# Routing in a two-block transformer kernel: groups of u between the searches, six gather buffers, sums brought together by DMA, two stored batches kept in their tiles

## The chip, the core and the metric

The kernel runs on one core of a Trainium2 chip. The core has five engines with queues of their own: TensorE (PE), VectorE (DVE), ScalarE (ACT), GpSimd (POOL) and SyncE (SP), which here only issues DMAs. The metric is the time of one execution on the device in microseconds; a kernel is told by the median of several executions. Lower is better.

## What is computed

The kernel computes two blocks of a transformer on 512 tokens of width 1024, all in float32. The change touches the last part of the second block alone, a product-key mixture of 128 x 128 experts (`peer_ffn` of the reference):

```python
q = (xb @ w_pq).reshape(tokens, 8, 2, 128)
s = einsum("thpd,hpnd->thpn", q, sub_keys)          # 8 heads x 2 halves x 128 keys
s_top, i_top = top_k(s, 16)                         # per half
cand = s_top[:, :, 0, :, None] + s_top[:, :, 1, None, :]
best, ci = top_k(cand, 16)                          # 16 of the pairs
e = i1 * 128 + i2                                   # expert numbers, from i_top and ci
gate = softmax(best)
act = gelu(einsum("thkd,td->thk", u_exp[e], x))
y = einsum("thk,thkd->td", gate * act, v_exp[e])
out = rmsnorm(x_res + gt2 * y, final_g)
```

`u_exp` and `v_exp` have 16384 rows of 1024 numbers (64 MB each).

## The kernel before

**Two ways through the experts.** The first 128 tokens (`NS`) take a sparse way: for each of 4 groups of 32 tokens (`NG`) and 32 steps, an indirect DMA on the POOL queue gathers 128 rows of 4 KB from `u` (`sparse_u`, L1387) and later from `v` (`sparse_v`, L1678), and DVE multiplies and sums each gathered tile in one instruction (L1405 for u, L1697 for v). The other 384 tokens (`ND`) take a dense way: TensorE multiplies all of `u` with the tokens, ACT applies the gelu, the result is weighted with a matrix `W` that holds each token's gates at its experts (zero elsewhere), and TensorE multiplies that with all of `v`.

**Exact products.** A float32 product is made of three fp32r products of 128x384 or 128x512 (`mm3`, L194 to L196) of a high and a low part. ACT makes the high part (L148), DVE or POOL the low one by a subtraction (L149), both in `split`.

**A group of u** is one call of `expert_early` (L1417): `expert_parts` loads 512 KB of `u` through the SP queue (L1357) into one of three tiles `uraw` and splits it into `uhl` (three tiles of the tag "wlo"); `expert_u` runs 24 products and a gelu (L1366) into one quarter of a tile `ga`. There are 128 groups in 32 batches of four. A full `ga` is stored to `GAd` by the ACT queue (L1428) and loaded again later (L1650). Batch 31 (`N_EARLY`) isn't stored: it is computed at the start of the v stage. `ahead` holds the parts that are prepared early, here one group ahead of the products.

**The stages**, in the order of the program:

1. *Scores and searches* (to about 1294 us): products of `w_pq`; `top16` on DVE finds the 16 best of each half.
2. *Routing*, a loop over four tiles of 128 tokens (L1498): DVE builds the pairs `cand`, searches them (eight calls of `top16`, one for each head), takes differences for the softmax (L1522), ACT applies Exp (L1523), and eight rounds `h` of one-hot products `eq` (L1534, L1538) and sums (L1544) turn the found places into expert numbers `ei`. In six of the eight rounds (all but `H_SKIP`) one group of u is called, with POOL as the engine of the low part; four more (`E_LAST`) follow the loop. `pick` transposes `ei` and `gate` on TensorE, and DVE and ACT (L1489) copy them out. `share` sends both through DRAM for the sparse tokens after the first tile (L1380 to L1384).
3. *Marks*: 48 units of eight tokens. DVE (L1584) and ACT (L1585) make one-hot matrices from the picks, TensorE multiplies them (L1604), ACT copies the result to `stage`, which is stored to `Wd`. In each unit some two groups of u run and some three steps of `sparse_u` are taken, which the two `while` conditions at the end of the loop meter out. DVE makes the low parts here.
4. *v*: for each of 32 batches (`order`), `prepare` loads `W` (`Wt`, L1646), `ga` and 2 MB of `v` (L1656) and splits them; `products` runs 96 matmuls of 128x384 into eight banks of PSUM that stay open to the end. Between them `sparse_v` is stepped by a condition with `57`.
5. *End*: the last batch is multiplied bank by bank; after bank 3 the sparse tokens are ended. Their sums lie in `fin` on 128 partitions, four partitions for a token; eight matmuls with a 0/1 matrix `FOLD` (L1710) add the four. Then the norm and the output.

**Who sets the order.** The program is written in the tile language: a planner at build time puts the instructions of each engine in order by its own estimate of times, within the data dependences. `tc.keep_in_program_order` pins an instruction behind the one traced before it on the same engine. On the chip every engine and every DMA queue then runs strictly in that order, so an instruction that waits holds all behind it.

## Time and profile before

| what | value |
|---|---|
| median of three executions | 2561.01 us (2559.43 to 2565.94) |
| profiled execution, whole | 2564.41 us |
| its span, first to last instruction | 2562.4 us |
| busy: PE, DVE, ACT, POOL | 2452.3, 1753.2, 1159.9, 509.8 us |
| mean granted clock of TensorE | 0.979 of full speed |
| moved by DMA | 545.79 MB |

All rows below come from the profiled execution. A view by stretches shows for each engine its busy time and, in brackets, its instructions, then the granted clock and the DMAs' share of time and rate. A view of waits shows which instruction waited for which: in total, how often, and the longest. A timeline shows start, duration, engine, line, operation, written tile and read tiles, and in square brackets how long the engine had been idle and what ended that. All times are microseconds; "mean ns" is nanoseconds.

### The profile page before, as it was taken

What the parts mean: (1) busy time and instruction counts of PE and PEld (TensorE: products, weight loads), DVE (VectorE), ACT (ScalarE), POOL (GpSimd) and SP (SyncE); (2) the same over time, 40 slices, a digit from 0 to 9 for tenths busy, and PEclk for the clock granted to TensorE, in tenths of its full rate; (3) what the DMA queues carried; (4) which work ended last, traced back from release to release, by engine and by line L of the source; (5) the groups of instructions that cost most, each with busy time, mean ns of one, the idle gap of its engine ahead of it and who ended that gap; (6) DMA issues with size and microseconds to landing.
All of it is one profiled execution on the core that took longest, in us unless ns stands there. A gap on an engine that the chain in (4) does not pass through costs nothing.

```text
span 2562.4 us, 36881 instructions
## 1 busy us (share of the span) xinstructions
PE 2452.3 (96%) x13565; PEld 2241.0 (87%) x13565; DVE 1753.2 (68%) x4163; ACT 1159.9 (45%) x2339; POOL 509.8 (20%) x389
## 2 busy tenths in 40 slices
PE   8899989999999999999997889999999999999998
PEld 7789878888878888888896789999999899999997
DVE  6467687643374567446889777777773588888884
ACT  7346464323244445224232467767675333333333
POOL 0021000000000000000043344434420144445430
PEclk9899999999999999999998889999999999999999
DMA  8511347742332221334133589999996999999981
GB/s 299 183 63 34 112 154 274 256 171 91 107 131 104 94 87 65 111 132 160 62 101 101 169 323 345 351 345 335 338 332 232 332 340 365 366 370 359 367 302 58
DMA packets 181905, 545.79 MB, mean 213 GB/s; under 512 B 17259, under 2 KB 68003, under 8 KB 170972
## 3 DMA queue, kind: packets, MB, share of 16 engines
q1 hardware_dynamic: 130592, 353.52, 40.0%
q0 software_dynamic: 38944, 139.49, 14.6%
q10 hardware_dynamic: 12188, 50.44, 5.0%
q8 instruction: 106, 1.74, 0.3%
q14 instruction: 75, 0.61, 0.1%
HBM read 480.25 MB, written 67.33 MB: 214 GB/s over the span
## 4 chain that ended last, share of the span: by engine, by line
PE 71%; DVE 10%; issue 9%; POOL 5%; DMA 3%; ACT 2%; POOLq 0%; SPq 0%; DVEq 0%; ACTq 0%
PE bank L196 21%; PE bank L194 21%; PE bank L195 20%; POOL gu L1375 5%; DVE eq L1534 1%; PE bank L1604 1%; DMA gu<-in_u_rows,eS 1%; PE bank L732 1%; PE bank L324 1%; PE bank L735 1%; DVE best L1544 1%; PE bank L323 1%; DMA adaw<-in_w_adaT 1%; PE bank L1164 1%; DVE eq L1538 1%
## 5 line engine op out<-in xcount | busy, mean ns | idle before, releaser
L194 PE MATMUL bank<-hTh,uhl 128*128 128x384 f32 x1024 | 357.7, 349 | 33.8 <-ACT uhl L148 33.8
L196 PE MATMUL bank<-hTh,uhl 128*128 128x384 f32 x1024 | 355.0, 347 | 23.9 <-DVE uhl L149 12.3
L195 PE MATMUL bank<-hTl,uhl 128*128 128x384 f32 x1024 | 352.1, 344 | 0.0
L196 PE MATMUL bank<-wah,vlo 128*128 128x384 f32 x1024 | 347.2, 339 | 0.0
L194 PE MATMUL bank<-wah,vhi 128*128 128x384 f32 x1024 | 346.0, 338 | 0.0
L195 PE MATMUL bank<-wal,vhi 128*128 128x384 f32 x1024 | 344.7, 337 | 0.0
L194 PE MATMUL bank<-hTh,whi 128*128 128x512 f32 (+1 forms) x832 | 318.4, 385 | 1.2 <-ACT hTh L148 1.2
L195 PE MATMUL bank<-hTl,whi 128*128 128x512 f32 (+1 forms) x832 | 315.4, 380 | 1.7 <-DVE hTl L149 1.7
L196 PE MATMUL bank<-hTh,wlo 128*128 128x512 f32 (+1 forms) x832 | 314.9, 379 | 0.2 <-DVE wlo L177 0.2
L1375 POOL DMA_INDIRECT gv<-in_v,eS x107 | 172.3, 1610 | 346.4 <-DVE sacc L1697 182.4
L194 PEld LDWEIGHTS bank<-hTh,uhl 128*128 128x128 f32 x1024 | 198.5, 194 | 36.0 <-ACT uhl L148 36.0
L1375 POOL DMA_INDIRECT gu<-in_u_rows,eS x128 | 178.6, 1395 | 255.1 <-DVE sr L1405 244.4
L196 PEld LDWEIGHTS bank<-hTh,uhl 128*128 128x128 f32 x1024 | 197.9, 193 | 30.9 <-DVE uhl L149 16.2
L148 ACT ACTIVATE wah<-ga 128x384 fp32r<-128x384 f32 x128 | 66.1, 518 | 349.7 <-PE bank L196 343.3
L195 PEld LDWEIGHTS bank<-hTl,uhl 128*128 128x128 f32 x1024 | 198.3, 194 | 0.0
L149 DVE TENSOR_TENSOR wlo<-wraw,whi 128x512 fp32r<-128x512 f32 (+1 forms) x200 | 129.5, 685 | 93.4 <-ACT whi L148 93.1
L196 PEld LDWEIGHTS bank<-wah,vlo 128*128 128x128 f32 x1024 | 192.4, 188 | 0.5 <-issue 0.5
L194 PEld LDWEIGHTS bank<-wah,vhi 128*128 128x128 f32 x1024 | 192.3, 188 | 0.2 <-issue 0.2
L195 PEld LDWEIGHTS bank<-wal,vhi 128*128 128x128 f32 x1024 | 192.1, 188 | 0.2 <-issue 0.2
L195 PEld LDWEIGHTS bank<-hTl,whi 128*128 128x128 f32 x832 | 158.9, 191 | 32.4 <-DVE hTl L149 2.6
L196 PEld LDWEIGHTS bank<-hTh,wlo 128*128 128x128 f32 x832 | 158.4, 190 | 32.4 <-DVE wlo L177 0.6
L194 PEld LDWEIGHTS bank<-hTh,whi 128*128 128x128 f32 x832 | 157.8, 191 | 32.0 <-ACT hTh L148 2.2
(508 smaller groups left out, 5221.0 us busy)
## 6 DMA issues: line engine op xcount, KB each, us to landing
uraw<-in_u SPq DMA_DIRECT2D x128, 512.0 KB, 6.6
vraw<-in_v SPq DMA_DIRECT2D x64, 1024.0 KB, 6.3
adaw<-in_w_adaT SPq DMA_DIRECT2D x48, 512.0 KB, 4.1
Wd<-stage ACTq DMA_DIRECT2D x48, 512.0 KB, 6.5
Wt<-Wd SPq DMA_DIRECT2D x32, 768.0 KB
GAd<-ga ACTq DMA_DIRECT2D x31, 768.0 KB
ga<-GAd SPq DMA_DIRECT2D x31, 768.0 KB, 9.6
wraw<-in_ffn_gu SPq DMA_DIRECT2D x22, 1024.0 KB, 6.6
```

The source lines that it names most:

```text
L148: nc.scalar.activation(hi, src, AF.Copy)
L149: (eng or nc.vector).tensor_tensor(lo, src, hi.bitcast(F32), op=OP.subtract)
L194: nc.tensor.matmul(o, l[0], r[0], start=start, stop=False)
L195: nc.tensor.matmul(o, l[0], r[1], start=False, stop=False)
L196: nc.tensor.matmul(o, l[1], r[0], start=False, stop=stop)
L323: nc.tensor.matmul(o, Q, K[:, g], start=True, stop=False)
L324: nc.tensor.matmul(o, Q, K[:, 2 + g], start=False, stop=stop)
L732: nc.tensor.matmul(o, slot[:, 0, ts(i)], v(i, 0), start=i == 0, stop=i == j)
L735: nc.tensor.matmul(o, slot[:, 1, ts(i)], v(max(0, j - 2) + i, 1), start=i == 0, stop=i == nb - 1)
L1164: nc.tensor.matmul(O[:, 128 * j + 64 * g:128 * j + 64 * g + n], pt[:, ts(i)], va[:, i, 128 * c + 64 * g:128 * c + 64 * g + n], start=i == ...
L1375: tc.keep_in_program_order(nc.gpsimd.indirect_dma_start(out=dst, out_offset=None, in_=src, in_offset=bass.IndirectOffsetOnAxis(ap=eS[:, g, ...
L1534: nc.vector.scalar_tensor_tensor(eq[:, a % 8], cf, float(offs[a]), step[:, :, a:a + 1].to_broadcast([128, 8, 16]), op0=OP.is_ge, op1=OP.mult)
```

## The change

In the routing loop a group of u is called after every second search (`E_TOP`, heads 1, 3, 5, 7) and in every second round (`E_PAIR`), eight for each tile, and one after the loop instead of four: 33 groups instead of 28 come before the marks. Parts are prepared two groups ahead. Exp moves into round 0, pinned; the copy of `gp` goes from ACT to DVE; the sum of the gates moves from round 1 to round 5; `share` moves to the second tile. `sparse_u` loads its `hr` in the third tile, into the two tiles of the tag "wraw", and gathers into six buffers instead of three: both "xs", `gu3`, and the three of the tag "P2". Both one-hot matrices of a unit lie in one tile of the tag "whi". The last two stored batches (29 and 30) are not stored but kept in the two `ga` tiles, and follow batch 31 in the order of v. The meters change: `sparse_u` ends one unit later, `sparse_v` takes 139 steps where it took 133 in the same time. The four quarters of the sums are moved by 16 DMAs of 32 partitions (128 KB each) onto the tokens' partitions and added by DVE; the matrix `FOLD` and its matmuls go.

```diff
-H_SKIP = 3, 7
-E_LAST = 4
+E_TOP = 1, 3, 5, 7
+E_PAIR = 0, 2, 4, 6
+E_LAST = 1
...
-        w2 = [wpool.tile([128, 2, D], F32, name=f"gu{i}", tag="wraw", bufs=2) for i in range(2)]
-        free = [w[:, i] for w in w2 for i in range(2)]
-        hr = [xsp.tile([128, D], F32, name="hr", tag="xs") for g in range(min(NG, XS))] + free[:max(0, NG - XS)]
-        bufs = free[max(0, NG - XS):] + [up.tile([128, D], F32, name="gu3")]
-        nb = len(bufs)
+        w2 = [wpool.tile([128, 2, D], F32, name=f"hr{i}", tag="wraw", bufs=2) for i in range(2)]
+        hr = [w[:, i] for w in w2 for i in range(2)]
         for g in range(NG):
             nc.sync.dma_start(hr[g], ap(Hd, 32 * g * D, [[0, 4], [D, 32], [1, D]]))
+        yield
+        bufs = [xsp.tile([128, D], F32, name="gu", tag="xs") for _ in range(XS)] + [up.tile([128, D], F32, name="gu3")]
+        bufs += [up.tile([128, D], F32, name="gu4", tag="P2", bufs=3) for _ in range(3)]
+        nb = len(bufs)
...
-        while len(ahead) < min(2, N_EARLY * BT - n):
+        while len(ahead) < min(3, N_EARLY * BT - n):
...
         if n % BT == BT - 1:
-            nc.scalar.dma_start(GAd[n // BT], early[1].rearrange("p a t -> p (a t)"))
+            if n // BT < N_EARLY - 2:
+                nc.scalar.dma_start(GAd[n // BT], early[1].rearrange("p a t -> p (a t)"))
+            else:
+                kept.append(early[1])
...
-            nc.scalar.activation(gp, o[:, 128:256], AF.Copy)
+            nc.vector.tensor_copy(gp, o[:, 128:256])
...
             for h in range(8):
                 top16(cand[:, h, :], best[:, h, :], ci[:, h, :])
+                if h in E_TOP:
+                    expert_early(nc.gpsimd)
...
-            nc.scalar.activation(gate, gate, AF.Exp)
...
-                if h == 1:
+                if h == 0:
+                    tc.keep_in_program_order(nc.scalar.activation(gate, gate, AF.Exp))
+                if h == 5:
                     nc.vector.reduce_sum(zs, gate, axis=AX.X)
...
-                if h not in H_SKIP:
+                if h in E_PAIR:
                     expert_early(nc.gpsimd)
+                if h == 1 and shared:
+                    share(*shared.pop())
+                if t == 2 and h == 1:
+                    next(sparse)
...
             if t == 0:
-                share(ei, gate)
+                shared.append((ei, gate))
...
-            G1 = wpool.tile([128, 8, 128], F32, name="G1", tag="whi", bufs=3)
-            P2 = up.tile([128, 8, 128], F32, name="P2", bufs=3)
+            both = wpool.tile([128, 2, 8, 128], F32, name="marks", tag="whi", bufs=3)
+            G1, P2 = both[:, 0], both[:, 1]
...
-            while 32 * NG + 6 > fed[0] and fed[0] * (units - 4) < (n + 1) * (32 * NG + 6):
+            while 32 * NG + 9 > fed[0] and fed[0] * (units - 3) < (n + 1) * (32 * NG + 9):
...
-        order = [N_EARLY] + [b for b in range(128 // BT) if b != N_EARLY]
+        order = [N_EARLY, N_EARLY - 2, N_EARLY - 1] + list(range(N_EARLY - 2))
...
+            if N_EARLY > b >= N_EARLY - 2:
+                ga = kept[b - N_EARLY + 2]
+            else:
+                ga = ga_tile() if batches[0] % 3 else pool.tile([128, BT, ND], F32, name="ga3")
             batches[0] += 1
-            ga = ga_tile() if batches[0] % 3 else pool.tile([128, BT, ND], F32, name="ga3")
-            if b < N_EARLY:
+            if b < N_EARLY - 2:
                 nc.sync.dma_start(ga.rearrange("p a t -> p (a t)"), GAd[b])
...
-            for f in range(2):
-                c = slice(f * 512, (f + 1) * 512)
-                o = bank()
+            for q in range(4):
                 for g in range(NG):
-                    nc.tensor.matmul(o[:NS], FOLD[:, g * NS:(g + 1) * NS], fin[:, g, c], start=g == 0, stop=g == NG - 1)
-                nc.vector.tensor_tensor(row[:, c], o[:NS], row[:, c], op=OP.mult)
-                nc.vector.tensor_tensor(x[:, c], x[:, c], row[:, c], op=OP.add)
+                    nc.sync.dma_start(parts[q][32 * g:32 * g + 32], fin[32 * q:32 * q + 32, g])
+                yield
+                if q % 2:
+                    nc.vector.tensor_tensor(parts[q], parts[q], parts[q - 1], op=OP.add)
+            sq = parts[1]
+            nc.vector.tensor_tensor(sq, sq, parts[3], op=OP.add)
+            nc.vector.tensor_tensor(sq, sq, row, op=OP.mult)
+            nc.vector.tensor_tensor(x, x, sq, op=OP.add)
...
-                while n >= 1 and vfed[0] * 57 < k * (32 * NG + 5):
+                while n >= 1 and vfed[0] * 57 < k * (32 * NG + 11):
```

## Rows read from the trace of the kernel before

**Rows 1.** Engines by stretch: routing, start of marks, marks, middle of v.

```profile
core 0: us, PE busy (x) PEld busy (x) DVE busy (x) ACT busy (x) POOL busy (x), PEclk, DMA share, GB/s
1294.00:1446.00 152.00, 119.76 (x601) 115.29 (x600) 151.86 (x639) 53.75 (x86) 55.69 (x24) 0.87 0.37 115
1446.00:1486.00 40.00, 27.48 (x163) 26.43 (x163) 21.02 (x47) 16.40 (x35) 18.16 (x12) 0.88 0.71 249
1486.00:1980.00 494.00, 489.46 (x3033) 486.46 (x3032) 346.88 (x694) 342.08 (x730) 169.56 (x121) 0.99 0.90 325
2060.00:2440.00 380.00, 380.00 (x2169) 380.00 (x2168) 321.35 (x377) 127.92 (x180) 177.78 (x106) 1.00 1.01 365
```

**Rows 2.** What PE waited for, 1294 to 1486 us.

```profile
PE bank L194 <- ACT uhl L148: 32.2, 7, 10.6
PE bank L196 <- POOL uhl L149: 11.5, 7, 2.1
```

**Rows 3.** What ACT waited for, 1300 to 1480 us, and the four Exps.

```profile
ACT gp L1489 <- DVE eI L1488: 45.3, 4, 14.4
ACT gate L1523 <- DVE gate L1522: 32.2, 4, 12.2
...
L1523 ACT ACTIVATE gate<-gate x4: 309/310/312, 1321.5 to 1422.4; 128x128 f32<-128x128 f32 x4
```

**Rows 4.** What the SP queue waited for, 1294 to 1486 us.

```profile
SPq L1381 <- DVE gate L1557: 14.9, 1, 14.9
...
SPq L1395 <- DVE cf L1551: 10.9, 1, 10.9
```

**Rows 5.** Timeline of routing: POOL's low parts and DVE beside them.

```profile
1324.68 7.19 POOL L149 TENSOR_TENSOR uhl<-uraw,uhl 128x1024 fp32r<-128x1024 f32 x3 [10.33 <-ACT uhl L148]
...
1327.11 2.50 DVE L1557 TENSOR_TENSOR gate<-gate,zs 128x128 f32<-128x128 f32 x1
```

**Rows 6.** DVE by line, 1290 to 1450 us, and the four L1557.

```profile
L1534 DVE SCALAR_TENSOR_TENSOR eq<-cf,step 128x128 f32<-128x128 f32 x64 | 28.0, 498 | 0.0
L1538 DVE SCALAR_TENSOR_TENSOR eq<-cf,tf 128x128 f32<-128x128 f32 x64 | 15.4, 306 | 0.0
...
L1557 DVE TENSOR_TENSOR gate<-gate,zs x4: 278/2464/2500, 1327.1 to 1428.2; 128x128 f32<-128x128 f32 x4
```

**Rows 7.** Timeline of ACT: two gelus of groups run back to back.

```profile
1302.08 0.49 ACT L1366 ACTIVATE ga<-bank 128x384 f32<-128x384 f32 x1 [2.73 <-PE bank L196]
...
1306.24 0.49 ACT L1366 ACTIVATE ga<-bank 128x384 f32<-128x384 f32 x1 [2.72 <-PE bank L196]
```

**Rows 8.** Timeline from the end of routing into the marks.

```profile
1446.10 0.28 DVE L1553 SCALAR_TENSOR_TENSOR ei<-first,ei 128x128 f32<-128x128 f32 x1
...
1460.79 1.95 PE L1604 MATMUL bank<-G,P 128*128 128x128 f32 x16
...
1470.20 1.23 DVE L1405 CUSTOM_DVE_ANT_0 gu<-gu,hr 128x1024 f32<-128x1024 f32 x1 [9.16 <-DMA gu<-in_u_rows,eS]
...
1485.24 0.47 ACT L1366 ACTIVATE ga<-bank 128x384 f32<-128x384 f32 x1
```

**Rows 9.** Waits in the marks: DVE 1446 to 1980 us, PE 1486 to 2004 us.

```profile
DVE gu L1405 <- DMA gu<-in_u_rows,eS: 112.4, 64, 9.2
...
PE bank L196 <- DVE uhl L149: 12.3, 8, 3.7
```

**Rows 10.** Timeline of DVE at the start of v.

```profile
1996.19 0.56 DVE L1662 TENSOR_TENSOR ga<-ga,Wt 128x384 f32<-128x384 f32 x1 [3.02 <-DMA ga<-GAd]
```

**Rows 11.** DMA issues by line.

```profile
vraw<-in_v SPq DMA_DIRECT2D x64, 1024.0 KB, 6.3
...
ga<-GAd SPq DMA_DIRECT2D x31, 768.0 KB, 9.6
```

**Rows 12.** The chain that ended last, 2500 us to the end.

```profile
2528.25 3.53 PE bank L1710 x8
2532.65 3.62 PE bank L1710 x8
```

More of the change, by code (lines that the diff above doesn't have):

```diff
@@ L1343, in tile_body @@
     Wd = dram.tile([ND // 32, 128, 128, 32], F32, name="Wd")
-    GAd = dram.tile([N_EARLY, 128, BT * ND], F32, name="GAd")
+    GAd = dram.tile([N_EARLY - 2, 128, BT * ND], F32, name="GAd")
     Ed = dram.tile([2, NS, 128], F32, name="Ed")
@@ L1402, in sparse_u @@
                 s, g = steps[k - nb + 1]
-                b = bufs[(k + 1) % nb]
+                b = bufs[(k - nb + 1) % nb]
                 d = sr[:, 2, g, s:s + 1]
@@ L1413, in tile_body @@
     early = [0, None]
+    kept = []
     ahead = []
@@ L1434, in tile_body @@
         off += 16 // (a + 1)
-    assert off == N_PAIR
+    assert off == N_PAIR and NG == 4
     with ExitStack() as ph:
@@ L1473, in tile_body @@
         wk = routing.enter_context(tc.tile_pool(name="rw", bufs=1))
-        picks, found = [], []
+        picks, found, shared = [], [], []
         sparse = sparse_u()
@@ L1627, in tile_body @@
         nc.sync.dma_start(gfc, A["final_cols"])
-        order = [N_EARLY] + [b for b in range(128 // BT) if b != N_EARLY]
+        order = [N_EARLY, N_EARLY - 2, N_EARLY - 1] + list(range(N_EARLY - 2))
+        assert 128 // BT == N_EARLY + 1
         first, last = order[0], order[-1]
@@ L1699, in sparse_v @@
                 yield
-            x, row, sq = (b[:NS] for b in bufs[:3])
-            FOLD = bufs[4][:, :NG * NS]
-            nc.sync.dma_start(FOLD, A["fold"])
+            parts, (x, row) = bufs[:4], bufs[4:6]
             ssq = small.tile([128, 1], F32, name="fsq", bufs=1)
@@ L1705, in sparse_v @@
             nc.sync.dma_start(row, ap(Mv, 5 * D, [[0, NS], [1, D]]))
-            for f in range(2):
-                c = slice(f * 512, (f + 1) * 512)
-                o = bank()
+            for q in range(4):
                 for g in range(NG):
-                    nc.tensor.matmul(o[:NS], FOLD[:, g * NS:(g + 1) * NS], fin[:, g, c], start=g == 0, stop=g == NG - 1)
-                nc.vector.tensor_tensor(row[:, c], o[:NS], row[:, c], op=OP.mult)
-                nc.vector.tensor_tensor(x[:, c], x[:, c], row[:, c], op=OP.add)
+                    nc.sync.dma_start(parts[q][32 * g:32 * g + 32], fin[32 * q:32 * q + 32, g])
[6 more added lines that the diff above has]
+            nc.vector.tensor_tensor(x, x, sq, op=OP.add)
             yield
-            nc.vector.memset(ssq, 1.0)
-            nc.scalar.activation(sq, x, AF.Square, accum_out=ssq[:NS])
+            nc.scalar.activation(sq, x, AF.Square, accum_out=ssq)
             nc.sync.dma_start(row, ap(A["final_g"], 0, [[0, NS], [1, D]]))
             r = inv_rms(ssq, D, newton=True)
-            nc.vector.scalar_tensor_tensor(x, x, r[:NS], row, op0=OP.mult, op1=OP.mult)
+            nc.vector.scalar_tensor_tensor(x, x, r, row, op0=OP.mult, op1=OP.mult)
             nc.sync.dma_start(out[0:NS, :], x)
@@ L1832, in lay_out @@
     a["cst"], a["t5"] = constants()
-    a["fold"] = (np.arange(128)[:, None] % 32 + 32 * (np.arange(NG * NS) // NS) == np.arange(NG * NS) % NS).astype(np.float32)
     a["x"] = i["x"][0]
```

## The prediction

> **What bounds the kernel now.** I read the view by stretches first. TensorE is the bound nearly everywhere: it is busy for 489 of the 494 us of the marks and for all of the middle of v, at full clock [rows 1]. The exceptions are the routing, where it is busy for 120 of 152 us, and the 40 us behind it, where it is busy for 27; both run at a granted clock of 0.87 to 0.88 [rows 1]. In the routing DVE is busy without a gap (151.9 of 152 us) [rows 1], so routing lasts as long as DVE's work, and what TensorE does meanwhile is free. Each group of u that fits there shortens the marks by its own time.
>
> Next I read who TensorE waits for there: for high parts that ACT makes (32.2 us) and for low parts that POOL makes (11.5 us) [rows 2]. Neither engine is full: ACT is busy for 54 us of 152, POOL for 56 [rows 1]. So I read what ACT itself waits for: 45.3 us in front of the copy of `gp` and 32.2 us in front of the four Exps, both for DVE [rows 3]. ACT runs in order, so splits and gelus of u stand behind these waits, up to 14.4 us at a time. The SP queue has the same fault: `share` waits 14.9 us for the gate and an `hr` load 10.9 us for a tile that the routing still reads [rows 4], with loads of u behind them.
>
> **The change part by part.** *Price of a group.* Two gelus of groups that run back to back start at 1302.08 and 1306.24 [rows 7]: 4.16 us of TensorE for each. The products of one unit of marks take 1.95 us [rows 8].
>
> *What is left to do.* Counting gelus, 30 groups and two units are done at 1485.24 [rows 8]. What then remains of the marks is 94 x 4.16 + 46 x 1.95 = 480.7 us of TensorE. After the change 33 groups are done when the first unit starts, and 91 x 4.16 + 48 x 1.95 = 472.2 us remain. So the question is when that first unit starts.
>
> *Routing.* The Exps of the first and last tile are at 1321.5 and 1422.4: 33.6 us of DVE for each tile [rows 3]. Eight groups are 33.3 us of TensorE, so they just fit beside it. What held them goes: the copy of `gp` leaves ACT and costs DVE 0.28 us a tile, by another copy-sized operation of 128x128 [rows 8]; `share` is issued when its data are there; `hr` goes into tiles that have long been free. Exp still waits for DVE, but it is now pinned behind four groups of its tile, and two groups beyond them are prepared, 8.3 us of cover for TensorE. Moving the sum of the gates to round 5 gives DVE the same work later, at no cost as long as Exp is done by then. From 1294 us 33 groups need 33 x 4.16 = 137 us, to 1431: that leaves over 20 us for the waits that stay, so DVE sets the end.
>
> DVE pays for the added low parts. While POOL makes three of them in 7.19 us, an operation of DVE with two inputs takes 2.50 us [rows 5] that takes 0.28 alone; three of the four are stretched so [rows 6], 3 x 2.2 = 6.6 us. The 64 operations of L1534 take 28.0 us, the 64 of L1538 in the same form 15.4 [rows 6]: 12.6 us more. That is 19.2 us for the 24 low parts of the loop, 0.8 us each. Two more for each tile make 1.6 us, 35.2 us a tile, 6.4 us in all. From both sides: nothing, if the groups in `E_TOP` run beside searches, which have one input; or, if all eight hold DVE for their whole 2.4 us, 8 x 2.4 - 4.8 = 14.4 us a tile. I take 0.8, the measured mean; the placement speaks for less, the steadier POOL for more.
>
> So the last `ei`, now at 1446.1 [rows 8], comes at 1452.5. I put the first unit at 1455, an estimate: `pick` has to be transposed before it. The gain is (1485.2 - 1455) + (480.7 - 472.2) = **39 us**; with no extra hold 46, with every hold in full a loss of 12.
>
> The Trainium skill (SBUF — State Buffer, section "Who interferes with whom") speaks against this part: it states that a VectorE instruction with two SBUF inputs and a GpSimd instruction that reads SBUF exclude each other for the whole instruction. The stretched operations above agree with that, 2.50 against 0.28 us. It also says that one input doesn't contend, which would make the groups beside the searches free. Taken as a full hold for every low part it is the second rival below.
>
> *Marks.* With three buffers DVE waited for gathers 64 times, 112.4 us, and low parts of u stood behind it: TensorE waited 12.3 us for them, the last part of that at the start of v [rows 9]. Six buffers put five gathers ahead of the first reduction; DVE no longer waits 9.16 us for the first, as at 1470 [rows 8]. I take **4 us**. The ends: 8 us gained if all waits of the marks go; 5 us lost if six transfers in flight delay loads of u, by the size of the waits of now. The meters keep the rate: a unit carries 2.84 gathers and 1.9 groups where it carried 2.9 and 2, and gets shorter by the group's share.
>
> *Start of v.* The second wait of DVE there, 3.02 us for the stored batch [rows 10], goes with the kept tiles, and a low part of u stood behind it. The wait for `Wt` stays, it depends on the last store of the marks. I take **3 us**, between 0 and 6.
>
> *Middle of v.* TensorE runs 2169 matmuls in 380 us, 175 ns each, so a batch of 96 takes 16.8 us, while the DMAs move 365 GB/s at a share of 1.01 [rows 1]. A batch loads 0.79 MB of `Wt`, 0.79 of `ga` and 2.1 of v [rows 11]; gathers of 0.52 MB come at 2 x 133/57 for each batch now and 2 x 139/57 then. That is 6.11 and 6.23 MB, 364 and 371 GB/s. The new demand is 1.6% over what the DMAs moved on average; over 27 batches that is 7 us if 365 is the most they can do, and nothing if it is what they were asked for. The two kept batches save loads of 1.6 MB, 4 us. I take **2 us lost**, between 0 and 7.
>
> *End.* The two rows of L1710 lie on the chain that ended last, 3.53 + 3.62 us [rows 12]; they go, **7 us**. In their place come 16 moves on the SP queue and five additions and products on DVE, about 6 us by 1.23 us for a tile of that size [rows 8]. The meter puts them some four batches earlier, where DVE is busy for 321 of 380 us and TensorE has a batch of operands ready: cover for all of it. Behind the moves on the SP queue stand the loads of v for the last batches; the queue waits for the last sum and for the row of the final gain. If the cover fails, a wait of 10 us like those of [rows 4] lands on TensorE, and the part is worth nothing or loses 3 us.
>
> **Sum**: -39 - 4 - 3 + 2 - 7 = -51 us. The span of 2562.4 becomes 2511, the execution of 2564.4 becomes 2513; the median of the runs is 3.4 us under that execution, so **2510 us**.
>
> **The rivals.** *(1) It isn't fed as planned.* The planner orders ACT and SP by its own times, and only Exp is pinned. If a wait of DVE still lands in front of splits, half of the 39 us stays away: 2530 us. For it: all the waits of [rows 3] are of this kind. Against it: the longest kind is removed, not moved. 0.12.
>
> *(2) POOL holds DVE in full.* The tiles take 48 us, the routing eats its gain and 12 us more: 2561 us, no change. For it: the operations in [rows 5]. Against it: the mean of 0.8 us now. Halfway, 1.6 us a part, gives 8 us more a tile: 2536. 0.16 for somewhere from 2528 to 2553, 0.03 for no change.
>
> *(3) Slower: the pinned Exp ties DVE to TensorE.* Exp now waits for four groups of its tile, and the gates of round 5 wait for Exp. If gaps drop TensorE to its lower level of 1.2 GHz, eight groups take 66.6 us in place of 33.3 and DVE waits for them: 33 us a tile, 132 us in all, 2642. It makes the kernel slower once the mean clock of the loop lies so low that a tile takes 13 us more than forecast, 48 us, at 33.3/48 = 0.69. For it: 0.87 with gaps today [rows 1]. Against it: the gaps shrink, and TensorE is more than 20 us ahead. 0.04.
>
> *(4) The transfers of v bound it.* 7 us lost instead of 2, 2515 us. For it: a share of 1.01. Against it: TensorE has no gap there [rows 1]. 0.10.
>
> **How the numbers follow.** The forecast itself, 2495 to 2525, has 0.55. The range goes from 2490 (46 + 8 + 6 + 7 us and no loss in v is 67, with some room) to 2545 (lock halfway and v at its bound), which leaves out the worst of rivals 2 and 3. About 0.3% (8 us) is what a measurement of this kernel can tell from no change. Faster by more than that: the forecast, rivals 1 and 4 and most of 2, 0.93; within it 0.03; slower 0.04.
>
> **What would show it.** Right: 33 gelus before the first unit, which starts at 1450 to 1460; no wait of ACT for `gp`, at most four for Exp; the Exps 34 to 37 us apart; TensorE over 90% busy in routing at a clock near 0.95; no L1710, and the last products some 50 us earlier. Wrong: Exps over 40 us apart with operations of DVE of 2.5 us in rows; DVE waiting for ACT's Exp; gaps of TensorE in v, or waits of DVE for `ga`, `Wt` or gathers there; SP waiting in the last batches with TensorE idle behind it.

## The result and the profile after

The changed kernel takes **2518.8 us** (median of 4 runs, 2514.4 to 2521.2) against 2561.0 (4 runs, 2559.4 to 2565.9) measured beside it: a ratio of 0.9821, 95% interval 0.9805 to 0.9837. Forecast were 2510 us, in a range from 2490 to 2545. So 42 us were gained where 51 were forecast. The execution that was profiled is the fastest of the four, 2514.4 us with a span of 2512.3; the one of before was 3.4 us above its median. So the profiled pair shows 50 us where the medians show 42, and places below are compared with a few us of such spread in mind.

The engines by stretch, after: the first two stretches are those of [rows 1], the marks and the middle of v now end earlier. Columns are the length in us, then busy time and count of each engine, the granted clock of PE, the DMA share and GB/s.

```profile
core 0: us, PE busy (x) PEld busy (x) DVE busy (x) ACT busy (x) POOL busy (x), PEclk, DMA share, GB/s
1294.00:1446.00 152.00, 127.75 (x679) 124.75 (x678) 151.72 (x616) 58.18 (x94) 68.24 (x28) 0.90 0.39 124
1446.00:1486.00 40.00, 39.36 (x246) 39.16 (x245) 29.49 (x60) 23.97 (x46) 23.87 (x17) 1.00 0.85 310
1486.00:1932.00 446.00, 446.00 (x2811) 446.00 (x2810) 334.02 (x679) 320.33 (x700) 176.19 (x117) 1.00 0.91 341
1932.00:1965.00 33.00, 27.99 (x151) 27.02 (x150) 16.32 (x24) 13.04 (x22) 7.89 (x6) 0.90 0.96 307
2060.00:2400.00 340.00, 340.00 (x1941) 340.00 (x1940) 294.32 (x343) 116.37 (x164) 160.24 (x99) 1.00 1.01 369
```

Read it column by column against [rows 1]. In the routing PE went from 120 to 128 busy us only, with 28 low parts on POOL for 24. Behind it PE has no gap any more (39.4 of 40 us for 27.5), and in 446 us of marks there is none at all.

What was waited for, after: PE from 1294 to 1486 us, ACT from 1300 to 1480, DVE from 1446 to 1932 (us in total, times, longest).

```profile
PE bank L195 <- ACT uhl L149: 16.9, 4, 9.0
PE bank L197 <- POOL uhl L150: 7.3, 4, 2.1
```

```profile
ACT gate L1562 <- DVE gate L1530: 20.7, 2, 12.3
ACT marks L1598 <- DVE i L1499: 18.1, 1, 18.1
```

```profile
DVE gu L1407 <- DMA gu<-in_u_rows,eS: 4.4, 2, 4.1
```

The copy of `gp` is gone from ACT's list [rows 3], and Exp waits twice instead of four times. In its place stands a new wait of 18.1 us: ACT's marks of the first unit, which were put ahead of splits, wait for the picks of the second tile of tokens. In the marks, DVE's 112.4 us of waits for gathers [rows 9] are 4.4.

One line or operation at a time, after (durations min/median/max, first and last start): the cast `cf` that follows the last search of each tile, the gates that Exp waits for, the Exps, the marks' matmuls and the gathers of u; then the two one-hot lines of DVE from 1290 to 1450 us.

```profile
L1527 DVE CAST cf<-ci x4: 213/223/750, 1318.2 to 1421.5; 128x128 f32<-128x128 uint32 x4
L1530 DVE TENSOR_TENSOR gate<-best x4: 272/284/2309, 1318.0 to 1428.0; 128x128 f32<-128x128 f32 x4
L1562 ACT ACTIVATE gate<-gate x4: 310/310/312, 1318.3 to 1446.8; 128x128 f32<-128x128 f32 x4
L1617 PE MATMUL bank<-marks x768: 270/275/275, 1463.4 to 1923.7; 128*128 128x128 f32 x192
L1376 POOL DMA_INDIRECT gu<-in_u_rows,eS x128: 933/1679/1993, 1463.1 to 1849.3; - x128
L1545 DVE SCALAR_TENSOR_TENSOR eq<-cf,tf 128x128 f32<-128x128 f32 x64 | 25.7, 469 | 0.0
L1541 DVE SCALAR_TENSOR_TENSOR eq<-cf,step 128x128 f32<-128x128 f32 x64 | 25.1, 460 | 0.0
```

The casts of the four tiles lie (1421.5 - 1318.2)/3 = 34.4 us apart, where the kernel before has 33.6 (its L1519 starts from 1321.4 to 1422.3). They are the measure of DVE's pace here, since DVE's work between them is nearly the same in every run; in the changed kernel some 2.7 us of small operations (a pick, a gate) fall behind the last cast, and with them it would be 35.3. The gates and the Exps are no such measure: in the changed kernel the gates of the last two tiles stand behind one-hot products of their own tile, the last one 6.5 us behind its cast, and ACT comes to the last Exp 18.8 us after that. The 33 groups are done when the first unit starts, as planned, but at 1463.4 and not at 1455. A gather comes every (1849.3 - 1463.1)/127 = 3.04 us.

### The profile page after: what moved, and what is told of

Its sections match the earlier page's. It is cut to its first block, busy times and chain, and to the rows that moved or that the text cites. A ratio compares the mean times of both kernels' runs of the same rounds, so it can differ in the third digit from the quotient of the medians.

```text
span 2512.3 us, 36888 instructions
## 1 busy us (share of the span) xinstructions
PE 2431.9 (97%) x13549; PEld 2230.1 (89%) x13549; DVE 1752.7 (70%) x4161; ACT 1155.5 (46%) x2335; POOL 531.0 (21%) x395
## 4 chain that ended last, share of the span: by engine, by line
PE 88%; DVE 5%; issue 2%; DMA 2%; ACT 1%; POOL 0%; SPq 0%; DVEq 0%; ACTq 0%; POOLq 0%
PE bank L197 26%; PE bank L195 26%; PE bank L196 26%; PE bank L1617 3%; PE bank L733 1%; PE bank L325 1%; PE bank L736 1%; PE bank L324 1%; PE bank L1165 1%; DMA adaw<-in_w_adaT 0%; PE bank L259 0%; PE bank L709 0%; DMA Wt<-Wd 0%; PE bank L1472 0%; PE bank L1259 0%
## 5 line engine op out<-in xcount | busy, mean ns | idle before, releaser
L195 PE MATMUL bank<-hTh,uhl 128*128 128x384 f32 x1024 | 354.2, 346 | 19.1 <-ACT uhl L149 18.5
L197 PE MATMUL bank<-hTh,uhl 128*128 128x384 f32 x1024 | 349.6, 341 | 10.8 <-POOL uhl L150 7.3
L1376 POOL DMA_INDIRECT gu<-in_u_rows,eS x128 | 188.4, 1472 | 200.0 <-DVE sr L1407 175.2
L195 PEld LDWEIGHTS bank<-hTh,uhl 128*128 128x128 f32 x1024 | 195.8, 191 | 20.3 <-ACT uhl L149 20.1
L197 PEld LDWEIGHTS bank<-hTh,uhl 128*128 128x128 f32 x1024 | 195.4, 191 | 13.0 <-POOL uhl L150 8.9
```

The source lines that it names most:

```text
L195: nc.tensor.matmul(o, l[0], r[0], start=start, stop=False)
L197: nc.tensor.matmul(o, l[1], r[0], start=False, stop=stop)
L1376: tc.keep_in_program_order(nc.gpsimd.indirect_dma_start(out=dst, out_offset=None, in_=src, in_offset=bass.IndirectOffsetOnAxis(ap=eS[:, g, ...
```

## The experiments

Every edit is made to the changed kernel. Ratios are to the kernel before, with 95% intervals; line numbers move by one or two where an edit adds lines. e1 to e4 ran on one chip, e5 to e8 on a second and e9 to e12 on a third, each beside the kernel before (medians 2565.5, 2567.0, 2563.2 and, beside e12, 2561.9 us). The changed kernel itself ran only on the chip of e1 and on that of the result, so a difference of a few us between chips is uncertain, and the ratios go with the times.

**e1: the changed kernel again**, as the value that the other runs are set against.

> The changed kernel unaltered, as the mark for the three beside it. Theory: the gain splits, by the two traces, into about 30 us of routing, 10 us of marks, 3 us at the start of v and 7 us at the end; the profiled pair lies 50 us apart, the medians 42. Expected here: 2514 to 2521 us.

2517.1 us (5 runs, 2513.7 to 2518.8), 0.981 (0.979 to 0.983). The result stands: 48 us below the kernel before on this chip, where the first pair has 42. All nine runs of this kernel lie from 2513.7 to 2521.2.

**e2: the sums by matmul.**

```
-            for q in range(4):
+            for f in range(2):
+                c = slice(f * 512, (f + 1) * 512)
+                o = bank()
                 for g in range(NG):
-                    nc.sync.dma_start(parts[q][32 * g:32 * g + 32], fin[32 * q:32 * q + 32, g])
+                    nc.tensor.matmul(o[:NS], FOLD[:, g * NS:(g + 1) * NS], fin[:, g, c], start=g == 0, stop=g == NG - 1)
...
-                while n >= 1 and vfed[0] * 57 < k * (32 * NG + 11):
+                while n >= 1 and vfed[0] * 57 < k * (32 * NG + 5):
```

> The changed kernel with the sums of the sparse tokens added by FOLD on TensorE again and the meter of v back at 133 steps. Theory (the two rows of L1710 were on the chain that ended last): 7 us slower than the changed kernel, with the 16 fp32 passes back between the last products. Rival (the moved sums cost elsewhere what they save): within 2 us of it.

2525.1 us (2524.2 to 2529.2), 0.984 (0.983 to 0.986): 8 us more than e1. The chain that ended last shows the two rows of [rows 12] again, of the same length (start, us):

```profile
2490.19 3.53 PE bank L1727 x8
2494.60 3.62 PE bank L1727 x8
```

The 7.15 us of TensorE are the price, and the DMA moves that replace them cost nothing that can be seen: in the changed kernel PE waits 2.6 us in all behind 2420 us, none of it for them.

**e3: all 31 batches stored** and loaded again, in the old order.

```
-            if n // BT < N_EARLY - 2:
-                nc.scalar.dma_start(GAd[n // BT], early[1].rearrange("p a t -> p (a t)"))
-            else:
-                kept.append(early[1])
+            nc.scalar.dma_start(GAd[n // BT], early[1].rearrange("p a t -> p (a t)"))
...
-        order = [N_EARLY, N_EARLY - 2, N_EARLY - 1] + list(range(N_EARLY - 2))
+        order = [N_EARLY] + [b for b in range(128 // BT) if b != N_EARLY]
```

> The changed kernel with batches 29 and 30 stored and loaded again and v in the old order. Theory: TensorE waits some 3 us more at the start of v, for a low part that stands behind DVE's wait for the stored batch; 3 us slower. Rival (DMA of the middle of v is the bound): 1.6 MB more at 365 GB/s, 4 us in the middle, with gaps of TensorE there. Second rival: no difference.

2518.2 us (2516.4 to 2524.2), 0.982 (0.980 to 0.983): 1 us more than e1, no difference that can be measured. The stretch from 1932 to 1990 us, first with all batches stored, then in the changed kernel:

```profile
1932.00:1990.00 58.00, 51.39 (x288) 50.04 (x288) 26.79 (x38) 18.87 (x31) 6.23 (x6) 0.97 0.97 334
```

```profile
1932.00:1990.00 58.00, 52.99 (x294) 52.02 (x293) 27.53 (x42) 19.59 (x32) 7.89 (x6) 0.94 0.93 311
```

PE is busy for 1.6 us more with the kept tiles. What else DVE waits for there, `Wt`, both have. And the wait for a stored batch, which the kept tiles should take away, has only moved to the first batch that is loaded (DVE in the changed kernel):

```profile
1972.58 1.50 DVE L1679 TENSOR_TENSOR ga<-ga,Wt 128x384 f32<-128x384 f32 x3 [8.64 <-DMA ga<-GAd]
```

PE has no gap behind it.

**e4: three gather buffers**, with the meter that belongs to them (32 NG + 6).

```
-        bufs += [up.tile([128, D], F32, name="gu4", tag="P2", bufs=3) for _ in range(3)]
```

> The changed kernel with three gather buffers for u instead of six. Theory: DVE waits for gathers over 100 us in the marks again, low parts of u come late, and TensorE loses about 10 us there. Rival (the marks lost time only through the start after routing): within 2 us.

2565.4 us (12 runs, 2556 to 2574), 0.9995 (0.998 to 1.001). The **whole** gain is gone, where 10 us were expected. The marks of this run by stretch, what DVE and PE waited for from 1446 to 1990 us, and the marks' matmuls and the gathers of u, here and in the kernel before:

```profile
1486.00:1932.00 446.00, 411.05 (x2505) 406.94 (x2504) 326.71 (x673) 290.77 (x642) 172.37 (x122) 0.96 0.90 325
```

```profile
DVE gu L1406 <- DMA gu<-in_u_rows,eS: 125.0, 57, 5.8
```

```profile
PE bank L197 <- DVE uhl L150: 34.9, 11, 6.0
```

```profile
L1616 PE MATMUL bank<-marks x768: 270/275/275, 1470.1 to 1979.1; 128*128 128x128 f32 x192
L1376 POOL DMA_INDIRECT gu<-in_u_rows,eS x128: 935/1677/1988, 1469.8 to 1915.3; - x128
```

```profile
L1604 PE MATMUL bank<-G,P x768: 270/275/276, 1460.8 to 1964.6; 128*128 128x128 f32 x192
L1375 POOL DMA_INDIRECT gu<-in_u_rows,eS x128: 932/1677/1972, 1460.1 to 1892.8; - x128
```

PE stands still for 35 of 446 us and runs at a clock of 0.96. The marks' matmuls last from 1470.1 to 1979.1 us, 509 us for what the changed kernel does in 460 (1463.4 to 1923.7), 49 us more. (The first unit also starts some 5 us later than in e1, where it is at 1465.4; no run shows why.) The gathers of u come every 3.51 us. A buffer is free again only when DVE has reduced it, so three buffers give one turn of 3 x 3.51 = 10.5 us. A unit of marks with its 1.9 groups wants 1.95 + 1.9 x 4.16 = 9.85 us of TensorE and carries 2.98 gathers (134 steps of the meter in 45 units): 2.98 x 3.51 = 10.5 us. That is longer than its products, and it is TensorE that waits, for low parts that stand behind DVE's waits for gathers. So the ring sets the pace, and a shorter routing only makes TensorE wait more in the marks. The comparison with the kernel before fits: there the first gather starts 9.7 us earlier, and the marks end 14.5 us earlier, though more groups are left for them.

**e5: the routing of before**, in the rest of the changed kernel: six groups in `E_PAIR`, four behind the loop, `gp` copied by ACT, Exp not pinned, sum of the gates in round 1, `share` at once, parts prepared one group ahead. The loads of `hr` stay in the third tile.

```
-E_TOP = 1, 3, 5, 7
-E_PAIR = 0, 2, 4, 6
-E_LAST = 1
+E_TOP = ()
+E_PAIR = 0, 1, 2, 4, 5, 6
+E_LAST = 4
...
-            nc.vector.tensor_copy(gp, o[:, 128:256])
+            nc.scalar.activation(gp, o[:, 128:256], AF.Copy)
...
```

> The changed kernel with the routing of before (six groups for each tile in the rounds, four behind the loop, parts one ahead, gp and an unpinned Exp on ACT, share after the first tile); six buffers, sums by DMA and kept batches stay. The run with three buffers was no faster than the kernel before, so the ring of gathers bounded the marks. Theory A (the gain needs both: groups moved into routing and a ring that lets the marks get shorter): some 30 us slower than the changed kernel, about 2547 us, with ACT waiting for gp and Exp some 75 us again. Theory B (six buffers alone make the gain): within 8 us of the changed kernel.

2539.6 us (2538.8 to 2542.3), 0.990 (0.987 to 0.993): 22 us of the gain lie in the routing, once there are six buffers, where some 30 were expected. ACT's waits are back:

```profile
ACT gp L1495 <- DVE eI L1494: 49.5, 4, 14.4
ACT gate L1531 <- DVE gate L1530: 30.3, 3, 12.2
```

Its last matmul of the marks is at 1951.4 us, against 1964.6 before with three buffers and nearly the same routing (first unit at 1460.6 and 1460.8): 13 us that the buffers bring in the marks with the old routing.

**e6: four gather buffers** (32 NG + 7).

```
-        bufs += [up.tile([128, D], F32, name="gu4", tag="P2", bufs=3) for _ in range(3)]
+        bufs += [up.tile([128, D], F32, name="gu4", tag="P2", bufs=3) for _ in range(1)]
```

> The changed kernel with four gather buffers for u. With three, 128 gathers took 445 us, 3.5 us each, or 10.5 us for one turn of the ring. Theory A (latency over number of buffers): four buffers allow 2.6 us each, less than the 3.04 us at which the six run, so the time is within 5 us of the changed kernel, and DVE waits for gathers under 40 us. Theory B (the three tiles of the tag P2 or the longer queue matter by themselves): about halfway, 2540 us.

2525.6 us (2519.7 to 2526.5), 0.984 (0.981 to 0.987). One more buffer brings 40 of the 48 us between three and six. That is neither theory: not within 5 us of the changed kernel (8 by the times, 7 by the ratios), and far from halfway. The gathers come every (1870.2 - 1468.7)/127 = 3.16 us, and DVE still waits for some:

```profile
DVE gu L1407 <- DMA gu<-in_u_rows,eS: 40.5, 28, 5.4
```

**e7: no group of u beside the routing** (all 33 behind it). It tells how long DVE takes alone.

```
-E_TOP = 1, 3, 5, 7
-E_PAIR = 0, 2, 4, 6
-E_LAST = 1
+E_TOP = ()
+E_PAIR = ()
+E_LAST = 33
```

> The changed kernel with no group of u inside the routing loop and 33 behind it, to measure DVE's routing without POOL beside it. Theory (low parts on POOL hold operations of DVE with two inputs): the differences for Exp (L1530) of the first and last tile lie 28 to 30 us apart for each tile, where the changed kernel has 36.7, and the one-hot products take 0.21 us each. Rival (no hold, DVE's own work): 34 us or more. The time is not the point; some 60 us more than the changed kernel.

2574 us (one run). The casts `cf` of this run, and the stretch from the first to the last of them in the kernel before and in the changed one:

```profile
L1527 DVE CAST cf<-ci x4: 217/218/222, 1318.4 to 1392.0; 128x128 f32<-128x128 uint32 x4
```

```profile
1321.40:1422.30 100.90, 71.91 (x353) 68.36 (x352) 100.80 (x390) 30.09 (x41) 35.90 (x15) 0.85 0.35 107
```

```profile
1318.20:1421.50 103.30, 90.22 (x480) 88.05 (x479) 103.16 (x380) 35.91 (x48) 49.65 (x20) 0.92 0.45 143
```

Without POOL three tiles take 73.6 us, 24.5 each, less than the 28 to 30 of the theory. In the same stretch POOL makes 15 low parts in the kernel before and 20 in the changed one; by the program's six and eight for each tile it would be 18 and 24, but the planner lets some of them fall outside. So a low part on POOL costs DVE (100.9 - 73.6)/15 = **1.8 us** before and (103.3 - 73.6)/20 = **1.5 us** after (1.6 with the 2.7 us that fall outside), not 0.8.

**e8: ACT's marks of the first three units pinned** behind what the program issues before them.

```
+PIN = 3
...
+            pin = tc.keep_in_program_order if n < PIN else lambda ins: ins
...
-                    nc.scalar.activation(P2[:, k + i], IOTA, AF.Square, scale=-1.0, bias=i2[:, tok])
-                nc.scalar.activation(P2[:, k:k + 4], P2[:, k:k + 4], AF.Relu, scale=-1.0, bias=1.0)
+                    pin(nc.scalar.activation(P2[:, k + i], IOTA, AF.Square, scale=-1.0, bias=i2[:, tok]))
+                pin(nc.scalar.activation(P2[:, k:k + 4], P2[:, k:k + 4], AF.Relu, scale=-1.0, bias=1.0))
```

> The changed kernel with ACT's instructions of the first three units of marks pinned behind what is traced before them. In the changed kernel ACT waits 18 us for a number of the picks with splits of u behind it, and TensorE runs at 0.67 of its clock in those 20 us. Theory (that wait costs TensorE 9 us and the clock some 5 more): 8 to 14 us faster than the changed kernel, about 2507 us, unless DVE's routing sets the start of the marks anyway. Rival (DVE sets the start: the last picks come at 1464 us whatever ACT does): within 3 us.

2518.7 us (2515.2 to 2522.2), 0.982 (0.979 to 0.985): no change. The wait of 18 us is gone from ACT; PE still waits for ACT's high parts once for 9 us, and now for the routing itself (PE from 1294 to 1500 us):

```profile
PE bank L196 <- ACT uhl L150: 11.3, 3, 9.3
...
PE bank L1489 <- DVE gate L1567: 4.9, 1, 4.9
PE bank L1488 <- DVE ei L1561: 4.0, 1, 4.0
```

The first unit starts at 1464.6 us in place of 1463.4. Why nothing was won is seen on DVE. In the changed kernel ACT stands still from 1412.7 to 1430.7, so POOL makes no low part from 1415 to 1433, DVE runs undisturbed and the last `ei` is there at 1444.3. Pinned, the splits go on, POOL goes on, and the same operations of DVE stretch. The nine one-hots of the last tile and one mark, in the changed kernel and pinned (timeline of DVE: start, us):

```profile
1432.08 1.89 DVE L1545 SCALAR_TENSOR_TENSOR eq<-cf,tf 128x128 f32<-128x128 f32 x9
```

```profile
1442.29 2.42 DVE L1599 TENSOR_SCALAR marks<-cst,i,gp 128x128 f32<-128x128 f32 x1
1444.63 6.33 DVE L1546 SCALAR_TENSOR_TENSOR eq<-cf,tf 128x128 f32<-128x128 f32 x9
1458.59 0.28 DVE L1561 SCALAR_TENSOR_TENSOR ei<-first,ei 128x128 f32<-128x128 f32 x1
```

1.89 us become 6.33, and the last `ei` comes 14 us later. What PE gains from ACT it loses to DVE. PE meets these waits by its order alone: the first unit belongs to the second tile of tokens, whose picks are there at 1441 us, but in PE's queue it stands behind the transposes of the last tile (L1488, L1489). No run puts it ahead of them.

**e9: the low parts of the groups beside the routing on DVE** instead of POOL, for `E_TOP` and `E_PAIR`.

```
                 if h in E_TOP:
-                    expert_early(nc.gpsimd)
+                    expert_early(None)
...
                 if h in E_PAIR:
-                    expert_early(nc.gpsimd)
+                    expert_early(None)
```

> The changed kernel with the low parts of the 32 groups in the routing loop made by DVE instead of POOL. Without any groups the tiles of the routing follow each other by 24.5 us, with eight groups on POOL by 36.7: 1.5 us of DVE for each low part that DVE doesn't even make. Making one takes DVE 1.22 us. Theory (the hold is the price): 24.5 + 8 x 1.22 = 34.3 us a tile, the marks start some 8 us earlier, 6 to 10 us faster than the changed kernel, about 2510 us. Rival (a low part in DVE's queue comes too late for TensorE, which then waits for DVE): slower than the changed kernel by 5 us or more, with TensorE waiting for DVE's uhl in routing.

**2509.75 us** (5 runs, 2508.2 to 2511.8), 0.980 (0.978 to 0.981). All five runs lie below all nine of the changed kernel, the lowest median of the study: 7 to 9 us faster by the times, 4 to 7 by the ratios of e1 and of the result (0.981 and 0.982). The routing by stretch, DVE's lines from 1290 to 1450 us, and the casts:

```profile
1294.00:1446.00 152.00, 137.34 (x744) 134.93 (x742) 151.86 (x672) 66.10 (x104) 0.00 (x0) 0.93 0.42 138
```

```profile
L150 DVE TENSOR_TENSOR uhl<-uraw,uhl 128x1024 fp32r<-128x1024 f32 x31 | 37.6, 1217 | 2.1 <-ACT uhl L149 2.1
L1541 DVE SCALAR_TENSOR_TENSOR eq<-cf,step 128x128 f32<-128x128 f32 x64 | 14.1, 284 | 0.0
L1545 DVE SCALAR_TENSOR_TENSOR eq<-cf,tf 128x128 f32<-128x128 f32 x64 | 14.1, 284 | 0.0
```

```profile
L1527 DVE CAST cf<-ci x4: 218/220/220, 1322.1 to 1421.2; 128x128 f32<-128x128 uint32 x4
```

DVE makes 31 subtractions of 1.22 us more and is still faster, 33.0 us a tile in place of 34.4 (34.1 in e1): the one-hots need 28.2 us in place of 50.8. PE is busy for 137 us instead of 128, and the first unit starts at 1458.5, 5 to 7 us earlier than in the result and in e1.

**e10: low parts on POOL beside the searches, on DVE in the rounds.**

```
                 if h in E_PAIR:
-                    expert_early(nc.gpsimd)
+                    expert_early(None)
```

> The changed kernel with the low parts called between the searches on POOL and those called in the rounds on DVE. Theory (searches have one input and aren't held, the rounds have two): 24.5 + 4 x 1.22 = 29.4 us a tile if POOL's four really run beside searches, so TensorE's 33.3 us set the pace, and up to 12 us faster than the changed kernel. Rival (the place in the program doesn't decide beside what POOL runs, since splits follow TensorE's pace): 24.5 + 4 x 1.22 + 4 x 1.5 = 35.4 us a tile, within 5 us of the changed kernel.

2516.4 us (2509.5 to 2518.6), 0.981 (0.979 to 0.983): as the changed kernel. The casts are (1416.2 - 1321.7)/3 = 31.5 us apart, between the theory and its rival. The one-hots still take 35.1 us (18.7 and 16.4) and not 28.2, so parts meant for the searches run beside the one-hots as well. The faster tiles bring nothing, since PE waits 23.0 us for low parts of DVE; the first unit starts at 1465.6.

**e11: Exp pinned in round 3** of the next tile, not in round 0.

```
-                if h == 0:
+                if h == 3:
                     tc.keep_in_program_order(nc.scalar.activation(gate, gate, AF.Exp))
```

> The changed kernel with Exp pinned in round 3 instead of round 0. ACT waits 20 to 24 us for the gates of two tiles in the changed kernel, 16 at the longest, with splits behind it. Theory (that wait costs TensorE its longest gap): ACT's waits for the gate under 10 us and up to 8 us faster. Rival (DVE's routing sets the start of the marks): the wait goes, the time stays within 3 us.

2513.1 us (2509.9 to 2514.8), 0.980 (0.979 to 0.982): 2 to 6 us faster than the changed kernel by ratios and times, with runs of both between 2513.7 and 2514.8: no difference that is clear of the noise. ACT from 1300 to 1480 us:

```profile
ACT marks L1598 <- DVE i L1499: 23.5, 1, 23.5
...
ACT gate L1562 <- DVE gate L1530: 6.3, 2, 5.3
```

Exp's wait shrinks from 20.7 to 6.3 us and the one for the picks grows from 18.1 to 23.5; the first unit starts at 1463.2, as before the edit. PE's wait for ACT's high parts stays as well (16.4 us for 16.9, the longest 14.5 for 9.0), so the theory doesn't hold; if there is a gain, no place of the trace shows it.

**e12: the edits of e8, e9 and e11 together.**

> Three edits to the changed kernel together: the low parts of the groups in the routing on DVE (2509.75 us alone), Exp pinned in round 3 of the next tile (2513.06 us alone), ACT's marks of the first three units pinned (2518.74 us alone, no change). Theory, the gains add up: with the low parts on DVE its tile takes 33.0 us, PE is idle for 14.7 of 152 us, and a part of that is splits behind Exp on ACT; with Exp ready when ACT comes to it (its wait falls from 24 to about 6 us) and the 23 us wait for the picks gone too, PE loses 4 to 6 us less: 2504 to 2507 us, the Exps still 33 us apart, first unit near 1455. Rival: PE's idle time in that version is all waits for DVE's low parts (16 of 18 us), which stand in DVE's own order; an earlier free ACT changes nothing: 2508 to 2512 us, PE's waits for DVE uhl still about 16 us, first unit near 1458. Second rival: a later Exp makes the gate of the next tile late on DVE, which now also makes the low parts in order, so these come later too: over 2513 us, DVE waiting for the gate.

2516.7 us (2511.2 to 2518.8), 0.982 (0.980 to 0.984): 7 us slower than e9 alone. Neither the sum of the gains nor the first rival; over 2513 us, as the second, but not by its mechanism, since DVE waits for no gate. PE from 1294 to 1486 us:

```profile
PE bank L198 <- DVE uhl L151: 14.7, 11, 6.2
PE bank L1619 <- ACT marks L1601: 4.2, 2, 3.0
```

The waits for low parts are near what they were in e9 (16.3), and a new one of 4.2 us has come: with the pins the last Exp starts at 1446.3 (1435.0 in e9), only 12 of DVE's marks are made before 1450 us (23 in e9), and the marks are late. The first unit starts at 1462.5, 4.0 us later than in e9; 3.0 of these are the longer of the two new waits. The last matmul of the marks is 7.3 us later (1926.2 for 1918.9), the loss; of the 3.3 us beyond the late start the second wait is 1.2, and no place of the trace is found for the rest.

## Why the prediction was right, and where it was not

**The sum was right, its division was not.** Forecast were -39 for the routing, -4 for the marks, -3 for the start of v, +2 in v, -7 at the end. The profiled pair shows 30 for the routing: (1485.2 - 1463.4) + 8.5, with the two sums of the prediction for what is left. The runs give, by taking one part back at a time, routing 22 (e5), buffers 48 (e4), kept tiles 1 (e3), sums 8 (e2). That is more than the 48 us of the whole (e1), since routing and buffers need each other. By steps from before: the end and the kept tiles bring 9 us, the buffers with the old routing another 17 (48 - 9 - 22), the new routing another 22. With the new routing and three buffers (e4) nothing is left even of the 9, though the part behind the marks is as short there as in the changed kernel (587.9 and 588.6 us from the last matmul of the marks to the end, 597.8 before): the new routing on three buffers **lost** about 9 us. That the sum came out near is in part luck: the routing gave less than forecast, the marks and the middle of v more, and the dependence of the two large terms was not in the sum at all.

**The step that failed: the worth of the buffers.** The prediction read 12.3 us of PE's waits in [rows 9] and set the end of the gain there, at 8. But it had lowered TensorE's work in the marks by its own routing term. Before, a unit had 480.7/46 = 10.45 us of TensorE. The meter makes 134 steps in 44 units, 3.05 gathers each and not the 2.9 of the prediction, and with 128 gathers from 1460.1 to 1892.8 us, 3.41 each, that is 10.4 us: the two ran level. The meter ties the gathers to the units, so equal lengths alone don't show which of them sets the pace; the sign that the ring had no room left was that DVE waited for 64 of the 128 gathers, 112.4 us in all [rows 9]. Any routing term above a few us had to come with a check of the gathers' pace against the shorter unit. That the change brought six buffers hid the error.

**Routing: DVE's pace was right, its ground was not.** Forecast were 35.2 us a tile and the last `ei` at 1452.5. The casts lie 34.4 us apart (35.3 with what falls behind the last one), and the last `ei` came at 1444.3 (1446.3 in e1). But the price of 0.8 us of DVE for each low part was too small: it is 1.8 in the kernel before and 1.5 to 1.6 in the changed one (e7). The working counted the difference of L1534 and L1538 and three gates [rows 6], and took L1538 as undisturbed; alone both lines take 14.1 us in 64 (e9), and casts, the sums of candidates (10.8 us before, 4.7 in e7) and the gates are stretched too. That the pace was still right is luck: with five low parts more, three tiles took 2.4 to 5.1 us more, 0.5 to 1.0 for each, and 0.8 lies between; why the added parts cost less than the mean no run shows. The second rival (a hold in full) is refuted: it wanted 48 us.

The sign that the prediction named for this, Exps 34 to 37 us apart, did not come: they lie (1446.8 - 1318.3)/3 = 42.8 us apart, beyond the 40 named as wrong. That is the order in ACT's queue, where the last Exp stands behind splits, gelus and marks, and not DVE's pace. The other half of that sign came too: the longest one-hots took 2.5 us.

The Trainium skill (SBUF — State Buffer, section "Who interferes with whom") counts copies, casts and `tensor_scalar` among the operations that can exclude GpSimd, besides those with two inputs, and says that `tensor_reduce` never does on this chip. The traces agree: the mark in e8 is a `tensor_scalar` and took 2.42 us there, 0.33 beside no low part, while the reductions of 128x1024 take 1.96 to 2.00 us on average by line with POOL (changed kernel, 1290 to 1450 us) and 1.99 to 2.00 without (e9). So "beside the searches" is free only as far as no other operation of DVE falls there.

**Routing: what set its end.** The prediction said DVE, with TensorE 20 us ahead. In the profile it was TensorE: the last `ei` came at 1444.3, and PE then still had groups to do until 1463.4. The prediction gave it 137 us for 33 groups, to 1431; they took until 1463.4, since PE was idle for 24 of the 152 us of the routing and its clock was 0.90 there. That is the 8 us by which the first unit came later than the 1455 of the forecast. Here are PE's longest gap and its cause in the timeline:

```profile
1430.74 0.99 ACT L1598 ACTIVATE marks<-cst,i 128x128 f32<-128x128 f32 x3 [18.05 <-DVE i L1499]
```

```profile
1433.10 0.69 PE L195 MATMUL bank<-hTh,uhl 128*128 128x384 f32 x1 [9.03 <-ACT uhl L149]
```

This is the first rival, a wait of DVE put in front of splits, at a place that it had not named; in the profiled pair 9 of the 39 us stayed away, not half. PE over 90% busy at a clock near 0.95 was wrong: 84% at 0.90. But e8 shows that taking this wait away alone gains nothing: without it DVE ends 14 us later and the first unit starts at the same time. Both bounds lie within a few us. What shortened the routing was to give the low parts to DVE (e9), which fits the reading that their price in DVE's time holds up both; no run takes the two apart.

**Marks, as a place** gained about 10 us in the profiled pair, where 4 were forecast and 8 were the upper end: beside the work that went into the routing, PE lost 4.5 us in gaps and about 5 by 1% of its clock before [rows 1], and nothing after.

**Start of v**: 3 us forecast, 1 measured (e3). The wait for `Wt` stands first in both kernels (8.7 us with all batches stored, 7.5 with kept tiles), and PE's wait for the low parts behind it only goes from 4.1 to 3.5 us. The wait of DVE for a stored batch, 3.02 us in [rows 10], didn't go: it came later, with 8.64 us, where PE had no gap.

**Middle of v**: a loss of 2 us forecast, none found. PE is busy for 340 of 340 us with 175 ns a matmul, as before, while the DMAs move 369 GB/s, where the kernel before moved 365. So 365 was not the most they can do, and the fourth rival falls.

**End**: 7 us forecast, 8 measured (e2). Cover for the moves was there: they are issued from 2423.7 to 2444.1 us, and the additions run from 2450 to 2462, while PE has no gap.

**The third rival** (slower, Exp tied to TensorE at its lower level) didn't come: the tiles stayed at 34.4 us, the clock at 0.90, and DVE was busy for 151.7 of 152 us.

## What to carry to other kernels

When a stage is made shorter, compare the pace of every ring of buffers in the next stage with its new length before a gain is booked. A wait of an engine that is not the bound (here 112 us of DVE for gathers) tells that the next bound is near; it was worth more (48 us, e4) than the visible waits of the bound itself (12 us).

A helper engine is not free. Price its work by what it takes from the bound engine, with a run of the same loop without such work; if that is more than the bound engine would need for it, give the work back. Count the helper's instructions in the trace and not in the program, and measure the pace of a loop at a place that the planner cannot move: here the gates moved by up to 11 us and the Exps by up to 25 against the casts.

And removing a wait gains only if nothing else ends at the same time: in e8 the next thing in line was DVE's routing, and it took the whole gain.

## What was not expected of the hardware

A subtraction of 128x1024 on POOL of 2.4 us took 1.5 to 1.6 us from DVE in the changed kernel and 1.8 in the kernel before, on average over all that DVE does in the routing, while DVE makes the same subtraction in 1.22 us (e9). The helper cost more than it saved: 4 to 9 us of the kernel (e9).

The turn of a ring of indirect gathers of 0.52 MB, from one use of a buffer to the next, was 10.5 us with three buffers and 12.6 with four (4 x 3.16). With four it hardly bound any more: PE waited 5.7 us for low parts in the whole of the marks (e6), for 34.9 with three (e4). With six it was 18.2 us and bound nothing: PE had no gap in 446 us. Between three and four lay 40 us of the kernel.
